# Most of the FFN's down projection by seven half-size products, its activation forms passed through DRAM

## The chip, the cores and the metric

The kernel runs on one core of a Trainium2 chip. The metric is the device time of one execution in microseconds; lower is better.

## The reference

One transformer layer over 512 tokens (T) of width 2048 (D) in float32, and a last RMSNorm. Only the second half matters here:

```python
x  = x + concat(oA, oB) @ W_out                  # two attention-like mixers, not changed
h  = RMSNorm(x)
a  = causal_conv3(h @ w_gate) + conv_b           # 2048 -> 5632
x  = x + (silu(a) * (h @ w_up)) @ w_down         # 5632 -> 2048
y  = RMSNorm(x)
```

## The kernel before

Everything is kept transposed, features on the 128 partitions and the 512 tokens along the free axis, so 2048 features are KT = 16 row blocks and 5632 are NF = 44. A float32 product is made of three matmuls on a split of each operand into a rounded part hi and a rest lo: hi·hi, hi·lo and lo·hi. The split of weights runs beside TensorE (PE): ScalarE (ACT) writes hi (`whi`, `fhi`), VectorE (DVE) subtracts it from the raw weights to get lo (`wlo`, `flo`).

The program is the mixers (to about 880 us of the span), the output projection, then three stages that the change touches.

**Gate and up.** For each of 44 row blocks f, gate and up together are a 2x2 product of half-size blocks, done with seven products in place of eight: sums of weight quarters (s1 to s4) meet seven forms of the activations (b11, n2, b21, t3, n1, n4, b22; `hforms`, held in SBUF). One product is 8 pairs of row blocks × 3 matmuls of 256 columns (L819 to L821), so a unit f has 168. Two of the weight sums are made by accumulating DMAs of POOL's queue (L765), two by DVE (L783), and `prepare` splits each of the seven weight tiles two products ahead. `glu(f)` runs the seven products, adds the partial results (L840 to L850), scales, convolves and gates (L851 to L858), splits the 128x512 activation (L860, L861) and stores both parts to DRAM (`actd`, L863, on the queue of SP).

**Down.** The activations come back from `actd` in four groups of GF = 11 row blocks (L886, POOL's queue). For each group and each of the 16 output blocks, `unit` runs 11 blocks × 3 matmuls of 512 columns (L201 to L203) into one PSUM tile, and DVE adds the tile to x1 in SBUF (L900). Weights `wdn` come on SP's queue (L142) and are split piece by piece (L149, L150).

**Late part and tail.** The last group of the last four output blocks is done with tokens on the partitions (L983 to L985), so that the final norm can start; what follows the last matmul is one norm step (L955 to L974) and the output stores.

Each engine executes its instructions in program order; a tile framework places the waits. An instruction on SP or POOL that issues a DMA waits there for what the DMA needs, and all later issues of the queue stand behind it. A stage's SBUF is handed on when its pools are closed, so the first tile of the next stage waits for the last reader of the old one.

Of the kernel before, what the change touches and what calls it, by code (L numbers as in the profile page):

```python
# [22 lines left out]
GF = 11  # L23
NG = NF // GF
# [12 lines left out]
NPIECE_D = NF * KT * P // PIECE  # L37
QH = T // 2
KP = KT // 2
FORM = KP * P  # L40
LEAD = 2
DMA_SUMS = True
# [11 lines left out]
def tile_hymba_block(ctx: ExitStack, tc: tile.TileContext, xT, wst, wgu, wdn, wfb, consts, out, out_t):  # L54
# [71 lines left out]
    class Stream:  # L126
# [7 lines left out]
        def make(self):  # L134
# [531 lines left out]
    x1d = dr.tile([KT, P, T], F32, name="x1d")  # L666
    actd = dr.tile([NF, 2, P, T], F32, name="actd")
# [18 lines left out]
    forms = {n: [] for n in NAMES}  # L686
    acc2 = tt.tile([P, T], F32, name="acc2")

    def form(name, j, src):
        pool = tt if j < KP - 1 else tl  # L690
        hi = pool.tile([P, QH], F32R, name=f"{name}h{j}")
        lo = pool.tile([P, QH], F32R, name=f"{name}l{j}")
        s.activation(hi, src, AF.Copy)
        v.tensor_tensor(lo, src, f32(hi), op=ALU.subtract)
        forms[name].append((hi, lo))

    def pair_forms(j, ha, hb):
        b11, b12, b21, b22 = ha[:, 0:QH], ha[:, QH:T], hb[:, 0:QH], hb[:, QH:T]
# [4 lines left out]
        form("b11", j, b11)  # L703
# [15 lines left out]
    def x1_out(d, ps):  # L719
# [3 lines left out]
        nc.sync.dma_start(out=x1d[d], in_=t)  # L723
# [10 lines left out]
    for d in range(WOPEN, KT):  # L734
        ps = MM()
        unit(ps, range(KT), os_)
        x1_out(d, ps)
    closed("wp", "wr", "pa")
    tl = opened("tl", 1)
    pair_forms(KP - 1, hg[-2], hg[-1])  # L740
    closed("xr")
    R2 = cp.tile([P, T], F32, name="R2", tag="R")
    nR2 = tl.tile([P, T], F32, name="nR2")

    def put2(u, r0, bc):
        s.activation(R2, bc, AF.Copy)
        s.activation(nR2, bc, AF.Copy, scale=-1.0)
# [3 lines left out]

    wf = opened("wf", 8)
    wh = opened("wh", LEAD + 2)
    gt = opened("gt", 1)
    ORDER = ("a11", "s2", "a12", "s3", "s1", "a22", "s4")
    raw = {}

    def W():
        return wf.tile([P, FORM], F32, name="wq", tag="wq")

    def load(f, name, q, q2=None):
        t = raw[f, name] = W()
        nc.sync.dma_start(out=t, in_=wgu[f, q])
        if q2 is not None:
            gp.dma_start(out=t, in_=wgu[f, q2], accum_op=ALU.add)  # L765

    def loads(f):

        if DMA_SUMS:
            load(f, "s1", 0, 1)  # L770
            load(f, "a11", 2)
            load(f, "s3", 0, 2)
            load(f, "a12", 3)
            load(f, "a22", 1)
        else:
            load(f, "a21", 0)
            load(f, "a22", 1)
            load(f, "a11", 2)
            load(f, "a12", 3)

    def add(f, name, x, y, into=None):
        t = raw[f, name] = W() if into is None else into
        v.tensor_tensor(t, raw[f, x], raw[f, y], op=ALU.add)  # L783

    def sums(f):
        if not DMA_SUMS:
            add(f, "s1", "a21", "a22")
            add(f, "s3", "a21", "a11", raw[f, "a21"])
        add(f, "s2", "s1", "a11")

    ready = {}
# [271 lines left out]
```

## Time and profile before

| | us |
|---|---|
| median of three runs | 2302.06 (2301.57 to 2303.62) |
| profiled execution, its own time | 2302.55 |
| span of the profiled execution | 2300.8 |
| gate and up, first to last matmul | about 905 to 1785 |
| down, from there to the last matmul | 1785 to 2290.8 |
| PE busy | 2273.4 (99%) |
| DVE, ACT, POOL busy | 1464.9, 939.2, 171.6 |

The profile is of one execution. Its span lies 1.75 us under that execution's own time, which holds what lies around the span; every "us from the start" is within the span. A busy PE is not PE at its peak: what a matmul costs is read from how many start in a stretch.

### The profile page before, as it was taken

The numbers are of one execution on the slowest core, as the hardware profiler recorded it, in microseconds if no ns is written. First come the engines' busy times: TensorE is split into PE (matmuls) and PEld (weight loads), VectorE is DVE, ScalarE is ACT, GpSimd is POOL, SyncE is SP. The second block draws the span as 40 slices with busy tenths as digits, with TensorE's granted clock in tenths as the row PEclk, the third lists the DMA queues.
The fourth block names the chain that finished last, engine by engine and source line by source line (L and its number), as shares of the span: only waits on it lengthen the run. The fifth ranks groups of instructions, "written<-read, shape, count | busy, mean of one in ns | idle before, by whom it ended". The sixth has DMA issues, their size and how long they took to land.

```text
span 2300.8 us, 34411 instructions
## 1 busy us (share of the span) xinstructions
PE 2273.4 (99%) x13662; PEld 2012.7 (87%) x13662; DVE 1464.9 (64%) x2194; ACT 939.2 (41%) x1484; POOL 171.6 (7%) x259
## 2 busy tenths in 40 slices
PE   8999999999999998999999999999999999999998
PEld 7888888788888887999999999999999788888886
DVE  6666467556457565888888888888887333333345
ACT  5333233334335454544444554454444222222234
POOL 4000000000000000000000000000000512000000
PEclk9999999999999999999999999999999999999999
DMA  5222322222222455877877887878784955223223
GB/s 177 83 83 83 100 74 96 74 83 80 86 83 74 142 163 177 226 212 207 216 215 214 212 212 209 216 200 222 208 217 136 375 198 196 92 97 99 85 100 110
DMA packets 112210, 352.67 MB, mean 153 GB/s; under 512 B 12816, under 2 KB 19088, under 8 KB 112048
## 3 DMA queue, kind: packets, MB, share of 16 engines
q1 hardware_dynamic: 89568, 272.67, 36.0%
q0 software_dynamic: 22336, 77.67, 15.4%
q8 instruction: 107, 1.75, 0.3%
q14 instruction: 55, 0.45, 0.1%
q10 hardware_dynamic: 144, 0.12, 0.0%
HBM read 318.96 MB, written 31.46 MB: 152 GB/s over the span
## 4 chain that ended last, share of the span: by engine, by line
PE 95%; DMA 2%; DVE 1%; issue 1%; ACT 0%; POOL 0%; DVEq 0%; ACTq 0%; POOLq 0%
PE pq L819 12%; PE pq L820 12%; PE pq L821 12%; PE mmt L201 9%; PE mmt L203 9%; PE mmt L202 9%; PE mxt L202 7%; PE mxt L201 7%; PE mxt L203 7%; PE mmt L286 2%; PE mmt L284 2%; PE mmt L285 2%; DMA ot<-actd 1%; DMA wq<-wgu 1%; DMA raw<-wdn 1%
## 5 line engine op out<-in xcount | busy, mean ns | idle before, releaser
L150 DVE TENSOR_TENSOR wlo<-raw,whi 128x512 fp32r<-128x512 f32 x453 | 316.3, 699 | 464.5 <-ACT whi L149 424.9
L149 ACT ACTIVATE whi<-raw 128x512 fp32r<-128x512 f32 x453 | 284.8, 630 | 686.3 <-PE mxt L202 322.2
L807 ACT ACTIVATE fhi<-wq 128x1024 fp32r<-128x1024 f32 x308 | 326.6, 1061 | 365.7 <-PE pq L820 323.0
L808 DVE TENSOR_TENSOR flo<-wq,fhi 128x1024 fp32r<-128x1024 f32 x308 | 376.3, 1222 | 58.2 <-ACT fhi L807 52.4
L201 PE MATMUL mmt<-at,whi 128*128 128x512 f32 x896 | 354.8, 396 | 0.0
L203 PE MATMUL mmt<-at,wlo 128*128 128x512 f32 x896 | 349.8, 390 | 0.0
L202 PE MATMUL mmt<-at,whi 128*128 128x512 f32 x896 | 349.3, 390 | 0.0
L201 PE MATMUL mxt<-ot,whi 128*128 128x512 f32 x660 | 262.2, 399 | 2.9 <-ACT whi L149 2.7
L202 PE MATMUL mxt<-ot,whi 128*128 128x512 f32 x660 | 261.8, 397 | 0.5 <-DMA ot<-actd 0.5
L203 PE MATMUL mxt<-ot,wlo 128*128 128x512 f32 x660 | 261.6, 397 | 0.5 <-DVE wlo L150 0.5
L203 PEld LDWEIGHTS mmt<-at,wlo 128*128 128x128 f32 x896 | 168.2, 188 | 35.9
L201 PEld LDWEIGHTS mmt<-at,whi 128*128 128x128 f32 x896 | 168.3, 188 | 34.9 <-issue 1.9
L202 PEld LDWEIGHTS mmt<-at,whi 128*128 128x128 f32 x896 | 168.4, 188 | 33.1
L201 PEld LDWEIGHTS mxt<-ot,whi 128*128 128x128 f32 x660 | 124.5, 189 | 34.8 <-ACT whi L149 2.9
L202 PEld LDWEIGHTS mxt<-ot,whi 128*128 128x128 f32 x660 | 124.6, 189 | 31.8 <-DMA ot<-actd 2.1
L203 PEld LDWEIGHTS mxt<-ot,wlo 128*128 128x128 f32 x660 | 124.7, 189 | 30.6 <-DVE wlo L150 1.0
L765 POOL DMA_DIRECT2D wq<-wgu x88 | 75.9, 862 | 782.1 <-DVE flo L808 388.1
L783 DVE TENSOR_TENSOR wq<-wq 128x1024 f32<-128x1024 f32 x88 | 107.5, 1222 | 3.5 <-DMA wq<-wgu 2.0
L286 PE MATMUL mmt<-wlo,at 128*128 128x512 f32 x256 | 100.6, 394 | 4.4 <-DVE wlo L150 4.4
L819 PE MATMUL pq<-b11h,fhi 128*128 128x256 f32 x352 | 100.2, 285 | 3.6 <-ACT fhi L807 3.6
L284 PE MATMUL mmt<-whi,at 128*128 128x512 f32 x256 | 101.7, 397 | 0.3 <-ACT whi L149 0.3
L821 PE MATMUL pq<-b11h,flo 128*128 128x256 f32 x352 | 99.9, 284 | 1.3 <-DVE flo L808 1.3
(303 smaller groups left out, 5067.7 us busy)
## 6 DMA issues: line engine op xcount, KB each, us to landing
wq<-wgu SPq DMA_DIRECT2D x220, 512.0 KB, 4.5
raw<-wst SPq DMA_DIRECT2D x143, 512.0 KB, 3.5
wq<-wgu POOLq DMA_DIRECT2D x88, 512.0 KB, 7.3
raw<-wdn SPq DMA_DIRECT2D x87, 512.0 KB, 3.5
ot<-actd POOLq DMA_DIRECT2D x88, 256.0 KB, 6.6
actd<-ah SPq DMA_DIRECT2D x44, 256.0 KB, 3.2
actd<-al SPq DMA_DIRECT2D x44, 256.0 KB, 3.0
xt<-xT SPq DMA_DIRECT2D x16, 256.0 KB, 5.3
```

Of the source, the lines that this page charges most:

```text
L149: s.activation(hi, src, AF.Copy)
L150: v.tensor_tensor(lo, src, f32(hi), op=ALU.subtract)
L201: pe.matmul(ps, lhsT=a, rhs=xh[:, ts], start=(first and i == 0), stop=False)
L202: pe.matmul(ps, lhsT=a, rhs=xl[:, ts], start=False, stop=False)
L203: pe.matmul(ps, lhsT=b, rhs=xh[:, ts], start=False, stop=(last and i == n - 1))
L284: pe.matmul(pss[i], lhsT=xh[:, ts], rhs=hi, start=(k == 0), stop=False)
L286: pe.matmul(pss[i], lhsT=xh[:, ts], rhs=lo, start=False, stop=(k == KT - 1))
L807: s.activation(hi, t, AF.Copy)
L808: v.tensor_tensor(lo, t, f32(hi), op=ALU.subtract)
L819: pe.matmul(ps, lhsT=a, rhs=th, start=(first and j == 0), stop=False, **kw)
L820: pe.matmul(ps, lhsT=a, rhs=tl, start=False, stop=False, **kw)
L821: pe.matmul(ps, lhsT=b, rhs=th, start=False, stop=(j == KP - 1), **kw)
```

## The change

Of the 44 row blocks that down contracts over, the first 36 (18 pairs) are now done by the same seven-product scheme; the last FL = 8 stay as they were, in one group.

- The 18 pairs are four chunks of 5, 5, 4 and 4 pairs (`CHUNKS`). For each chunk, eight units (pairs of output blocks, in the order `DORDER`) run seven products of n pairs × 3 matmuls of 256 columns. A unit's result goes to DRAM by an accumulating DMA of POOL (`yd`), 32 of 512 KB.
- The seven forms of the activations are made during gate and up, one pair for every two units (`forms_out`: four DVE operations, then splits into hi and lo), and stored to `formd` in DRAM instead of `actd` (1.8 MB a pair where two units stored 1.05 MB before). In down, a form of a chunk is loaded into one of ten slots (`df`, NDF = 10, 1.31 MB with n = 5) by two DMAs of SP's queue: seven for the chunk that runs, and three of the next one after its second unit's products; the other four are loaded during its last unit.
- The RMS factor R2 is no longer multiplied into the up half in `glu`. So yd holds down's sum without it, and its start value is x1/R2: eight times a load of 512 KB into one of two buffers `xi`, two DVE operations of 512 columns, a store of 512 KB, all in the first chunk and on POOL's queue.
- Down's weights come as four raw quarters a unit (wd7, SP's queue); all four sums are made by DVE (L796). Raw weights are loaded a unit ahead, in gate and up staggered over the unit's products.
- The order of the seven products is another one (`ORDER`, `NAMES`), with p5 as one more copy by ACT.
- The first unit of gate and up has DVE sums, and its loads and splits stand ahead of the last `x1_out` of the output projection.
- The last part has 8 blocks where it had 11: 96 late matmuls. `norm` waits 11 steps of the late loop (of 8 steps a row) before its ones-matmul, and multiplies out of place, three operations per row as before.

The core of the diff, with the functions that it adds:

```diff
-GF = 11
-NG = NF // GF
+FL = 8
+CHUNKS = (5, 5, 4, 4)
+NDF = 10
+DORDER = (6, 7, 0, 1, 2, 3, 4, 5)
...
-    ORDER = ("a11", "s2", "a12", "s3", "s1", "a22", "s4")
-    NAMES = ("b11", "n2", "b21", "t3", "n1", "n4", "b22")
+    ORDER = ("a11", "s2", "s1", "a12", "s3", "s4", "a22")
+    NAMES = ("b11", "n2", "n1", "b21", "t3", "b22", "n4")
...
+            elif self.units[u][2]:
+                when = {0: ("a11", "s1"), 2: ("a12",), 3: ("s3",), 4: ("a22",)}
+                self.loads(u + 1, *when.get(i, ()))
...
+    def forms_out(p, r):
+        c, j = next((c, p - at) for c, at in enumerate(STARTS) if p < at + CHUNKS[c])
+        v.tensor_tensor(r[:, 4], r[:, 0], r[:, 1], op=ALU.subtract)
+        v.tensor_tensor(r[:, 1], r[:, 3], r[:, 1], op=ALU.subtract)
+        yield KP // 2
+        v.scalar_tensor_tensor(r[:, 5], r[:, 4], -1.0, r[:, 3], op0=ALU.mult, op1=ALU.subtract)
+        v.tensor_tensor(r[:, 6], r[:, 5], r[:, 2], op=ALU.add)
+        for a, b in ((0, 4), (4, 7)):
+            parts_out(r[:, a:b], b - a, lambda i: formd[c][a:b, i, :, j].rearrange("s p t -> p s t"))
+            yield 6 * KP
...
-        v.tensor_tensor(uu, uu, nR2, op=ALU.mult)
         s.activation(t, t, AF.Silu)
         v.tensor_tensor(uu, uu, t, op=ALU.mult)
-        for i, part in enumerate((hi, lo)):
-            nc.sync.dma_start(out=actd[f, i], in_=f32(part))
+        if f >= 2 * NPAIR:
+            parts_out(r[:, b:b + 2], 2, lambda i: actd[f - 2 * NPAIR, i])
+        elif f % 2:
+            start(forms_out(f // 2, r))
...
+    with tc.high_priority():
+        sv.loads(first, "a11", "a21", "a22", "a12")
+        sv.prepare(7 * first)
+        sv.prepare(7 * first + 1)
+    for i in range(7):
+        chunk[0][NAMES[i]] = load_form(0, NAMES[i])
...
+    def down(c, k):
+        m = DORDER[k]
+        def after(i):
+            if c == 0 and i == 0:
+                if k + 1 < KP:
+                    load_x1(DORDER[k + 1])
+            if c == 0 and i == 2:
+                xi = x1s.pop(m)
+                v.scalar_tensor_tensor(xi[:, 0], xi[:, 0], -1.0, rms, op0=ALU.mult, op1=ALU.mult)
+                v.tensor_tensor(xi[:, 1], xi[:, 1], rms, op=ALU.mult)
+                gp.dma_start(out=yd[m], in_=xi)
+            if c + 1 < len(CHUNKS) and k == (1 if i < NDF - 7 else KP - 1):
+                chunk[c + 1][NAMES[i]] = load_form(c + 1, NAMES[i])
+        o = G("o", (P, 2, T), bufs=2)
+        seven(*(G(n, (P, QH)) for n in ("p1", "p5", "u2", "u3")),
+              o[:, 0, L], o[:, 0, H], o[:, 1, L], o[:, 1, H], chunk[c], after)
+        gp.dma_start(out=yd[m], in_=o, accum_op=ALU.add)
...
-    for g in range(NG - 1):
-        nxt = []
-        for d in range(KT):
-            ps = MX()
-            unit(ps, range(GF), acts)
-            v.tensor_tensor(x1[d], x1[d], ps, op=ALU.add)
-            if d < GF:
-                nxt.append(acts_of((g + 1) * GF + d))
-        acts = nxt
...
-        start(norm(i, ps, ys, 6 if i < 3 else 0))
+        start(norm(i, ps, FL + 3 if i < 3 else 0))
```

The change moves instructions on the queues. The first place is SP's queue at the end of gate and up, where down begins. `actd<-ah` and `actd<-al` are the stores of the last units' activations, `raw<-wdn` loads down's weights. Before:

```order
478 L863 DMA actd<-ah 128x512 [waits DMAHW2_49,Activation_49]
479 L863 DMA actd<-al 128x512 [waits DMAHW3_49,DVE_49]
480 L142 DMA raw<-wdn 128x512 [waits DMAHW4_49,PE_49]
481 L142 DMA raw<-wdn 128x512 [waits DMAHW5_49]
482 L142 DMA raw<-wdn 128x1024 [waits DMAHW6_49,PE_49]
483 L142 DMA raw<-wdn 128x1024 [waits DMAHW7_49]
484 L142 DMA raw<-wdn 128x1024 [waits DMAHW4_49,DMAHW5_49,DMAHW0_49,DVE_49]
485 L863 DMA actd<-ah 128x512 [waits DMAHW1_49,Activation_49]
486 L863 DMA actd<-al 128x512 [waits DMAHW2_49,DVE_49]
487 L142 DMA raw<-wdn 128x1024 [waits DMAHW6_49,DMAHW3_49,DVE_49]
```

The same place of the changed kernel; `wq<-wd` loads the raw quarters of down's second unit, `df<-formd` are halves of the forms of the first chunk, of which 14 stand here in all (rows 487 to 502 without the two stores):

```order
485 L786 DMA wq<-wd 128x640 [waits DMAHW1_49]
486 L786 DMA wq<-wd 128x640 [waits DMAHW2_49]
487 L969 DMA df<-formd_5879 128x1280 [waits DMAHW3_49,PE_49]
488 L969 DMA df<-formd_5879 128x1280 [waits DMAHW4_49]
489 L889 DMA actd<-oh 128x512 [waits DMAHW5_49,Activation_49]
490 L889 DMA actd<-ol 128x512 [waits DMAHW6_49,DVE_49]
491 L969 DMA df<-formd_5879 128x1280 [waits DMAHW7_49,PE_49,Pool_49]
492 L969 DMA df<-formd_5879 128x1280 [waits DMAHW0_49]
493 L969 DMA df<-formd_5879 128x1280 [waits DMAHW1_49]
494 L969 DMA df<-formd_5879 128x1280 [waits DMAHW2_49]
```

Two units' weights and the first form now stand ahead of the last stores, and the other six forms behind them; the wait for PE in row 491 is for the last product of gate and up. Behind row 502 follow the weights of the third unit (4 DMAs), three forms of the second chunk (6) and the weights of the fourth unit (4).

The second place is POOL's queue in the same stretch of the changed kernel, where `xi` are the two buffers of the start values:

```order
143 L788 DMA wq<-wgu 128x1024 [waits DMAHW5_49,DMASW2_49,DVE_49]
144 L992 DMA xi<-x1d_5868 128x1024 [waits DVE_49]
145 L992 DMA xi<-x1d_5869 128x1024 [waits PE_49]
146 L1005 DMA yd_5876<-xi 128x1024 [waits DMASW0_49,DVE_49]
147 L1005 DMA yd_5877<-xi 128x1024 [waits DMASW3_49,DMASW1_49,DVE_49]
148 L992 DMA xi<-x1d_5862 128x1024 [waits DMASW4_49,DMASW2_49]
149 L992 DMA xi<-x1d_5863 128x1024 [waits DMASW5_49,DMASW3_49]
150 L1005 DMA yd_5870<-xi 128x1024 [waits DMASW6_49,DMASW4_49,DVE_49]
```

Where the queue brought back activations before (11 pairs of `ot<-actd`, then 16 `ot<-x1d`), it now runs a chain: a load, two DVE operations, a store, and only then the next load into the same buffer.

The third place is DVE in down's first unit of the changed kernel. `flo` is the lo part of a product's weights, `wq<-wq` a sum of weights, `u` a partial result:

```order
1913 L825 TENSOR_TENSOR flo<-wq,fhi 128x640 [waits PE_49,Activation_49]
1914 L1003 SCALAR_TENSOR_TENSOR xi<-xi,rms 128x512 [waits DMASW0_49,DVE_49]
1915 L1004 TENSOR_TENSOR xi<-xi,rms 128x512
1916 L796 TENSOR_TENSOR wq<-wq 128x640 [waits DMAHW7_49]
1917 L912 TENSOR_TENSOR u_18276<-p_18274,pq 128x256 [waits DMAHW6_49,PE_49,Activation_49]
1918 L825 TENSOR_TENSOR flo<-wq,fhi 128x640 [waits Activation_49]
1919 L1003 SCALAR_TENSOR_TENSOR xi<-xi,rms 128x512 [waits DMASW1_49]
1920 L1004 TENSOR_TENSOR xi<-xi,rms 128x512
1921 L825 TENSOR_TENSOR flo<-wq,fhi 128x640 [waits PE_49,Activation_49]
1922 L1003 SCALAR_TENSOR_TENSOR xi<-xi,rms 128x512 [waits DMASW4_49,DMASW2_49,DVE_49]
1923 L825 TENSOR_TENSOR flo<-wq,fhi 128x640 [waits PE_49,Activation_49]
```

The operations on `xi` stand between the splits, and the third of them (row 1922) waits for a load that itself waits for the first store; the split in row 1923 stands behind it.

## Rows read from the trace of the kernel before

**Rows 1.** The page's head: span, and busy time of each engine.

```profile
span 2300.8 us, 34411 instructions
PE 2273.4 (99%) x13662; PEld 2012.7 (87%) x13662; DVE 1464.9 (64%) x2194; ACT 939.2 (41%) x1484; POOL 171.6 (7%) x259
```

**Rows 2.** The chain that ended last, by engine.

```profile
PE 95%; DMA 2%; DVE 1%; issue 1%; ACT 0%; POOL 0%; DVEq 0%; ACTq 0%; POOLq 0%
```

**Rows 3.** Four stretches: gate/up, transition, down's start, down.

```profile
core 0: us, PE busy (x) PEld busy (x) DVE busy (x) ACT busy (x) POOL busy (x), PEclk, DMA share, GB/s
1200.00:1400.00 200.00, 200.00 (x1692) 200.00 (x1692) 167.82 (x202) 100.57 (x121) 17.28 (x20) 1.00 0.80 213
1785.20:1815.00 29.80, 25.95 (x92) 18.21 (x92) 12.27 (x19) 8.58 (x14) 18.18 (x35) 0.89 1.00 368
1795.00:1845.00 50.00, 49.34 (x206) 37.91 (x205) 15.49 (x24) 11.38 (x18) 29.06 (x55) 1.00 1.03 395
2000.00:2100.00 100.00, 100.00 (x430) 80.48 (x429) 32.80 (x49) 22.75 (x36) 0.54 (x1) 1.00 0.29 96
```

**Rows 4.** Timeline of PE, last late matmuls: start, duration, instruction.

```profile
2287.81 0.39 PE L985 MATMUL mxt<-ot 128*128 128x512 f32 x1
...
2290.53 0.39 PE L985 MATMUL mxt<-ot 128*128 128x512 f32 x1
```

**Rows 5.** Timeline of PE around down's start; idle time in brackets.

```profile
1784.98 0.28 PE L821 MATMUL pq<-b22h,flo 128*128 128x256 f32 x1
1787.94 0.50 PE L201 MATMUL mxt<-ot,whi 128*128 128x512 f32 x1 [2.67 <-ACT whi L149]
...
1791.46 0.63 PE L203 MATMUL mxt<-ot,wlo 128*128 128x512 f32 x1
1791.89 0.63 PE L201 MATMUL mxt<-ot,whi 128*128 128x512 f32 x1
...
1795.29 0.39 PE L203 MATMUL mxt<-ot,wlo 128*128 128x512 f32 x1
```

**Rows 6.** SP's timeline there: issue, wait included, of DMAs.

```profile
1791.43 0.33 SPq L863 DMA_DIRECT2D actd<-ah  x1
1792.16 0.33 SPq L863 DMA_DIRECT2D actd<-al  x1
```

**Rows 7.** DVE by shape, 1200 to 1400: count, busy, mean ns.

```profile
L808 DVE TENSOR_TENSOR flo<-wq,fhi 128x1024 fp32r<-128x1024 f32 x71 | 86.8, 1222 | 12.9 <-ACT fhi L807 11.6
L855 DVE SCALAR_TENSOR_TENSOR t<-a,con,t 128x510 f32<-128x510 f32 x10 | 7.5, 750 | 0.4
L851 DVE TENSOR_TENSOR a<-a,R 128x512 f32<-128x512 f32 x10 | 6.9, 692 | 0.3
L840 DVE TENSOR_TENSOR u<-p,pq 128x256 f32<-128x256 f32 x10 | 4.2, 421 | 0.0
```

**Rows 8.** DVE's timeline at down's start, operations back to back.

```profile
1790.05 0.69 DVE L858 TENSOR_TENSOR uu<-uu,t 128x512 f32<-128x512 f32 x1
1790.66 0.69 DVE L150 TENSOR_TENSOR wlo<-raw,whi 128x512 fp32r<-128x512 f32 x1
```

**Rows 9.** DMA issues of the whole run: KB each, median us to landing.

```profile
wq<-wgu SPq DMA_DIRECT2D x220, 512.0 KB, 4.5
wq<-wgu POOLq DMA_DIRECT2D x88, 512.0 KB, 7.3
ot<-actd POOLq DMA_DIRECT2D x88, 256.0 KB, 6.6
ot<-x1d POOLq DMA_DIRECT2D x16, 256.0 KB, 6.9
```

**Rows 10.** PE's timeline between the output projection and gate/up.

```profile
897.48 0.39 PE L203 MATMUL mmt<-at,wlo 128*128 128x512 f32 x1
...
904.72 0.58 PE L819 MATMUL pq<-b11h,fhi 128*128 128x256 f32 x1 [3.63 <-ACT fhi L807]
```

**Rows 11.** DVE's timeline at the very end.

```profile
2290.95 0.69 DVE L955 TENSOR_TENSOR ot<-ot,mxt 128x512 f32<-128x512 f32 x1 [1.52 <-PE mxt L985]
2294.97 1.88 DVE L974 TENSOR_TENSOR ot<-ot,mxt 128x512 f32<-128x512 f32 x3
```

More of the change, by code (lines that the diff above doesn't have):

```diff
@@ L740, in tile_hymba_block @@
+    sv = Seven()
+    for f in range(NF):
+        sv.add([wgu[f, q] for q in range(4)], KP, f > 0)
+    sv.loads(0, "a11", "a21", "a22", "a12")
+    sv.prepare(0)
+    sv.prepare(1)
+    x1_out(KT - 1, ps)
     pair_forms(KP - 1, hg[-2], hg[-1])
@@ L758, in W @@
[L758 to L779, printed above, removed]
@@ L811, in product @@
-    def product(g, ps, first=True):
-        prepare(g + LEAD)
-        hi, lo = ready.pop(g)
-        rhs = forms[NAMES[g % 7]]
-        for j in range(KP):
-            a, b = hi[:, j * P:(j + 1) * P], lo[:, j * P:(j + 1) * P]
-            th, tl = rhs[j]
-            kw = {"skip_group_check": not first}
-            pe.matmul(ps, lhsT=a, rhs=th, start=(first and j == 0), stop=False, **kw)
-            pe.matmul(ps, lhsT=a, rhs=tl, start=False, stop=False, **kw)
-            pe.matmul(ps, lhsT=b, rhs=th, start=False, stop=(j == KP - 1), **kw)
-            step()
+    gt = opened("gt", 1, "right")
@@ L851, in glu @@
+        seven(*(G(n, (P, QH)) for n in ("p1", "p5", "u2", "u3")), a[:, L], a[:, H], uu[:, L], uu[:, H], hforms)
         v.tensor_tensor(a, a, R2, op=ALU.mult)
@@ new lines, in tile_hymba_block, with load_form @@
+    opened("wh", LEAD + 2)
+    wr = opened("wr", 2)
+    wp = opened("wp", 3)
+    dt = opened("dt", 1, "right")
+    gt = opened("gt", 1, "right")
+    def load_form(c, name):
+        n = CHUNKS[c]
+        t = dt.tile([P, 2, max(CHUNKS), QH], F32R, name="df", tag="df", bufs=NDF)
+        for i in range(2):
+            nc.sync.dma_start(out=f32(t[:, i, 0:n]), in_=formd[c][SLOTS.index(name), i])
+        return [(t[:, 0, j], t[:, 1, j]) for j in range(n)]
+    chunk = [{} for _ in CHUNKS]
+    first = len(sv.units)
@@ L878, in O @@
+    load_x1(DORDER[0])
+    for c in range(len(CHUNKS)):
+        for k in range(KP):
+            if c + 1 == len(CHUNKS) and k + 1 == KP:
+                while ws.made < 3:
+                    ws.make()
+            down(c, k)
+    closed("gt", "dt")
+    pq = opened("pq", 33, "right")
+    yp = opened("yp", 1, "right")
     def O(dt=F32, shape=(P, T)):
         return pq.tile(list(shape), dt, name="ot", tag="q")
-    A = X = O
-    def acts_of(f):
-        parts = (O(F32R), O(F32R))
-        for i, part in enumerate(parts):
-            gp.dma_start(out=f32(part), in_=actd[f, i])
-        return parts
@@ new lines, in tile_hymba_block @@
+    for f in range(FL):
+        acts.append((O(F32R), O(F32R)))
+        for i, part in enumerate(acts[-1]):
+            nc.sync.dma_start(out=f32(part), in_=actd[f, i])
+    ys = []
+    for d in (12, 0, 4, 8):
+        y4 = yp.tile([P, 4, T], F32, name=f"y{d}")
+        for b in range(2):
+            gp.dma_start(out=y4[:, 2 * b:2 * b + 2], in_=yd[d // 2 + b])
+        ys.append(y4)
+    y12, *ys = ys
+    ng3 = sm.tile([P, KT], F32, name="ng3")
+    v.tensor_scalar_mul(ng3, con[:, C_G3:C_G3 + KT], -1.0)
```

360 lines of the change are left out of this document (226 added, 134 removed).

## The prediction

> **What bounds the kernel now.** I read first the page's head: PE is busy for 2273.4 us of a span of 2300.8, the next engine, DVE, for 1464.9 [rows 1]. The chain that ended last is PE for 95% and DMA for 2% [rows 2]. So time is gained by fewer or shorter matmuls, and lost where PE waits; I cost the change stage by stage in matmuls and then look for new waits. The stretches give the price of a matmul: in gate/up 1692 of 256 columns start in 200.00 us, 0.1182 us each; in down 430 of 512 columns in 100.00 us, 0.2326 each [rows 3]; the late ones start 12 steps apart in 2290.53 − 2287.81 us, 0.2267 each [rows 4]. In both stages PE never idles; DVE has 16% to spare in gate/up and the DMA engines 20% (share 0.80) [rows 3].
>
> The one place where down waits today is its start. The last matmul of gate/up starts at 1784.98, the next at 1787.94 after 2.67 us of waiting, and then matmuls come 0.43 us apart, half clock (1.2 GHz), until about 1795.3 [rows 5]. Of the 29.80 us from 1785.2, the 92 matmuls need 92 × 0.2326 = 21.4, so this transition costs 8.4 us, with DMA engines full (share 1.00 at 368 GB/s; 395 GB/s right behind) [rows 3].
>
> **The matmuls.** Before, down has 4 × 16 × 11 × 3 = 2112, of which 132 are late: 1980 × 0.2326 + 132 × 0.2267 = 490.5 us. After: 4 chunks × 8 units × 7 products, together 8 × 7 × 18 × 3 = 3024 of 256 columns, 12 × 8 × 3 = 288 of 512, and 96 late: 357.4 + 67.0 + 21.8 = 446.2. **Saved: 44.3 us**, if the new stage runs as tightly as gate/up does.
>
> **Down's start.** Now count what must land there. T0 is the end of gate/up. Weights of two units and the first form wait for nothing late and are there. Six forms (6 × 1.31 = 7.9 MB) stand in SP's queue behind the stores of the last activations, which today are issued 6.5 to 7.2 us after the last matmul's start [rows 5, 6]; after the change the chain is shorter (no multiplication by nR2, DVE freer), say T0 + 3.5. At 0.38 MB/us, between the 368 and 395 GB/s of the full engines [rows 3], they need 21 us alone. POOL's chain shares the engines: eight loads and eight stores of 0.52 MB, two buffers. A 0.26 MB load of POOL took 6.6 to 6.9 us there [rows 9], so a buffer's turn (load, two DVE operations, store) takes about 15 us, and some 4 MB move in 30 us. The sixth form lands at about T0 + 3.5 + (7.9 + 4)/0.38 = T0 + 35. A unit's matmuls take 105 × 0.1182 = 12.4 us; the queue lets PE work on the second unit's first products meanwhile (36 of its 105 matmuls in program order), so at T0 + 35 some 15 to 17 us of work have been done: loss 18 to 20 us. Then SP brings the third unit's weights, three forms of the second chunk (3.9 MB), and the fourth unit's weights. All that must land before the fourth unit starts is 14.9 MB by SP, up to 8.4 MB of the chain and 1.5 to 2 MB of accumulation: 25 MB at 0.38 are 66 us, where PE alone would be there at T0 + 37: loss 29. With 6 MB of chain by then it is 22. I take **24 us** (nearer to the count of all bytes, since nothing in these rows moves more), bounds 12 (395 GB/s, the chain held back by its own waits) to 35 (368 GB/s and everything before the fourth unit). Today's 8.4 go: **+15.6**.
>
> The Trainium skill (DMA: Bandwidth & Descriptors, Where 436 GB/s comes from) says that transfers between HBM and SBUF are bound at about 358 GB/s per core. This trace disagrees, with 395 GB/s over 50 us. By the page the 25 MB would take 70 us and the loss would be some 4 us more.
>
> **Steady units of down.** DVE per unit with n = 5: seven splits and four sums of 640 columns, five combinations of 256. No row has 640; between 512 (0.692) and 1024 (1.222) the records give 0.825 and 0.421 for 256 [rows 7]: 11.2 us. Back to back they start closer, 0.61 apart for 512 [rows 8] (88% of the record), hence 9.9. PE needs 12.4. The first chunk adds two operations on `xi` (1.3). With n = 4: 11 × 0.692 + 5 × 0.421 = 9.7 by records, 8.6 by starts, against 84 × 0.1182 = 9.9. It fits by either, closely by records: **0**, bound +13 (0.4 us in each of 32 units, if the order makes splits late). DMA with n = 4 per unit: 1.05 MB of weights, 0.92 of the next chunk's forms (7.3 MB over eight units), 0.52 of accumulation, taken twice since it reads and writes: 3.0 MB, at 0.38 8 us of 9.9.
>
> **Between chunks** four forms (5.2 MB, with n = 4: 4.2) load during the last unit. With that unit's weights and accumulations about 8.8 MB have 21 us before the last form is used; at 0.38 it takes 23 for n = 5. Three boundaries: **+3**, bounds 0 and 8.
>
> **From down's seven to its rows.** The 16 loads of activations (4.2 MB) wait for SBUF that the last product frees, and beside them run 4.2 MB of y on POOL. That is the transition of today again, 8.4 us [rows 3], with as many bytes for the first rows but weights made ahead: **+9**, bounds 5 and 13.
>
> **Gate/up.** Per unit DVE loses two operations of 512 and gains half of four of 256, one of 1024 and one of 768: +0.5 us on 16.8 (167.82/200 of 19.9), still under PE. DMA gains 0.39 MB on 213 GB/s × 19.9 us = 4.2: share 0.80 becomes 0.87 [rows 3]. **0**, bound +8. At its start PE idles from 897.5 to 904.72 today with the split last [rows 10]; the first loads then come earlier but wait for SBUF of the last out-projection weights, and three sums are DVE's: **0**, ±2.
>
> **Tail.** After the last matmul today's chain runs 2290.95 to 2300.8; its three last multiplications take 1.88 [rows 11]. The 11-step gap exceeds the eight steps of a row, so the third row's multiplications stand in DVE's order behind the fourth's: **+2**, bounds 0 and 3.
>
> **Sum**, on the profiled execution's own time of 2302.55: −44.3 + 15.6 + 3 + 9 + 2 = −14.7, so 2287.8; it lies 0.5 over the median of 2302.06, so 2287.4 for that median.
>
> **Rivals.**
> (a) The start is covered better than I count: POOL's chain runs late, so that forms have the engines alone. For it speaks that DVE's split order holds the chain at each round (its own work is under 1.5 us a turn [rows 7], the rest is waiting); against it that stores and loads are queued whenever a buffer is free. Loss 12 in place of 24, and boundaries 0: 2272.
> (b) DVE decides in down's units: records of 9.7 against 9.9 leave 2%, and a split stuck behind an `xi` wait (the third place of the order) holds all behind it. +13: 2300. It decides when a unit's DVE work passes PE's 9.9.
> (c) The slow side: the new form stores write pieces of 1 KB per row and partition, where `actd` wrote 2 KB. No row of this kernel has such a store. If they cost double, the store's share (0.92 MB a unit, 2.4 us) becomes 4.8 us and the DMA share 0.80 − 0.07 + 0.24 = 0.97 [rows 3], and accumulated weights, which land in 7.3 us even at 0.80 [rows 9], come late by about 1 us in each of 36 units: 2323. It decides once the share reaches 1.0 over a unit. In a sentence apart: the Trainium skill (DMA: Bandwidth & Descriptors, Specifications) puts the least piece for full rate at 512 B, by which this rival does nothing; no row here shows it.
> (d) The clock stays at half during the start. Each product of a unit is 1.8 us of matmuls and a form arrives every 3.4 to 5, so PE works in bursts; today after 2.67 us of waiting it ran at half clock for 7 us [rows 5]. While PE waits for forms anyway, slow matmuls cost little; the price is the work after the last form, up to two units at half speed before the full clock is back: +12, 2299. The Trainium skill (TensorE: Matmul & The Clock Gate, HAM oscillation) describes just this, short bursts between DMA waits that all run at 1.2 GHz; the trace of before agrees once, at 0.89 granted over the transition.
>
> **How the numbers follow.** My sum's case 0.50 (2276 to 2298), (a) 0.18, (b) 0.09, (c) 0.13, (d) 0.10. Predicted 2287.5. The range of 8 in 10 reaches over (a), (b) and (d), and half-way to (c) because several bounds may add up: 2264 to 2312. A measurement here can tell 0.2%, 4.6 us, from no change. Faster than 2297.5: 0.47 + 0.18 and a third of (b) and (d), 0.71. Within: 0.12, from the rest of (b), (d) and my case. Slower: 0.17, (c) and sums of upper bounds.
>
> **What would show it.** Down's units at 12.4 and 9.9 us with PE without gaps confirm the matmul term. At gate/up's end, waits of PE for `df` over 20 to 35 us with a DMA share of 1.0, then again before the fourth unit. At the rows' start about 9 us with waits for `ot<-actd`. Gate/up units still at 19.9 us with a share near 0.87, else (c). Splits waited for in down's units mean (b); full DMA throughput with low granted clock after the sixth form, (d). The prediction is wrong if gate/up gets longer, or if the start loses under 12 or over 35 us.

## The result, and the profile after

The changed kernel takes 2391.47 us (2389.7 to 2394.68, four runs), the kernel before 2302.47: a ratio of 1.0388 (1.037 to 1.0406). It is 89 us slower, where 14.7 us less was forecast. One of all the runs below, of `bboth`, ran at a mean granted clock of 0.72 and took 2903.73 us; the ratios leave it out. The page's head and chain of the changed kernel:

```profile
span 2390.1 us, 37853 instructions
PE 2284.5 (96%) x14958; PEld 2083.1 (87%) x14958; DVE 1645.3 (69%) x2567; ACT 1028.4 (43%) x1671; POOL 155.0 (6%) x209
...
PE 70%; DMA 14%; DVE 10%; issue 3%; ACT 2%; SPq 1%; DVEq 0%; ACTq 0%; POOL 0%; POOLq 0%
```

PE is still nearly always busy, but the chain has changed: 14% and 10% of it are now DMA and DVE, which had 2% and 1% [rows 1, 2]. A chain through DVE and DMA in stages that the forecast had as pure matmul time is the first sign. The stretches show where; they are gate/up, the four chunks of down (each ends where the last combination of its eighth unit starts on DVE, L928), and the rows done as before:

```profile
core 0: us, PE busy (x) PEld busy (x) DVE busy (x) ACT busy (x) POOL busy (x), PEclk, DMA share, GB/s
903.20:1807.00 903.80, 891.99 (x7394) 887.06 (x7394) 732.19 (x924) 450.71 (x574) 74.22 (x86) 1.00 0.82 222
1807.00:1952.00 145.00, 115.80 (x848) 111.26 (x849) 100.75 (x158) 51.36 (x88) 14.61 (x23) 0.89 0.77 261
1952.00:2072.00 120.00, 109.90 (x873) 106.72 (x871) 81.73 (x130) 48.22 (x86) 6.78 (x8) 0.99 0.66 203
2072.00:2168.00 96.00, 84.46 (x640) 81.75 (x641) 68.07 (x127) 37.62 (x75) 6.84 (x8) 0.95 0.63 186
2168.00:2267.50 99.50, 88.21 (x669) 84.73 (x667) 65.61 (x122) 38.06 (x77) 7.36 (x9) 0.95 0.55 147
2267.50:2377.00 109.50, 100.38 (x413) 76.89 (x414) 47.13 (x89) 39.99 (x72) 4.58 (x8) 0.94 0.47 155
```

Gate/up lasts 903.8 us where it was 880.6. Each chunk should last as long as its matmuls, 8 × 105 × 0.1182 = 99.3 us with five pairs and 79.4 with four, and lasts 144.7, 120.0, 96.5 and 99.4. DVE's busy share in the last two is only 0.7, and the DMA engines' 0.6: nothing is full, so these look like waits in sequence, not a lack of any engine. The granted clock of 0.95 in these stretches comes from short spells at 1.2 GHz that follow waits of PE, such as the 2.8 us before 2115.7 and the 3.0 us before 2155.8.

What DVE does in the third unit of the last chunk of the changed kernel (start, duration, instruction, idle time before it):

```profile
2209.85 0.68 DVE L796 TENSOR_TENSOR wq<-wq 128x512 f32<-128x512 f32 x1
2210.45 0.41 DVE L928 TENSOR_TENSOR o<-u,pq 128x256 f32<-128x256 f32 x1
2210.79 1.29 DVE L825 TENSOR_TENSOR flo<-wq,fhi 128x512 fp32r<-128x512 f32 x2
2211.99 0.41 DVE L912 TENSOR_TENSOR u<-p,pq 128x256 f32<-128x256 f32 x1
2212.32 1.29 DVE L825 TENSOR_TENSOR flo<-wq,fhi 128x512 fp32r<-128x512 f32 x2
2218.32 1.42 DVE L796 TENSOR_TENSOR wq<-wq 128x512 f32<-128x512 f32 x2 [4.71 <-DMA wq<-wd]
2219.66 0.69 DVE L825 TENSOR_TENSOR flo<-wq,fhi 128x512 fp32r<-128x512 f32 x1
```

Two sums (L796) wait 4.71 us for raw weights, and the split that PE needs next (the last row) stands behind them. PE starts again right after that split:

```profile
2220.40 0.38 PE L847 MATMUL pq<-df,flo 128*128 128x256 f32 x1 [2.11 <-DVE flo L825]
```

The program's order, with the tiles' numbers, tells whose sums they are:

```
2258 L825 TENSOR_TENSOR flo_21493<-wq_21236,fhi_21492 128x512 [waits PE_49,Activation_49]
2259 L796 TENSOR_TENSOR wq_21653<-wq_21520,wq_21522 128x512 [waits DMAHW7_49,DMAHW6_49,DVE_49]
2260 L796 TENSOR_TENSOR wq_21520<-wq_21520,wq_21518 128x512 [waits DMAHW5_49,DVE_49]
2261 L825 TENSOR_TENSOR flo_21514<-wq_21375,fhi_21513 128x512 [waits PE_49,Activation_49]
```

The split in row 2261 opens the unit with raw weights 21375 and following; the sums before it belong to the unit after that one (21518 to 21522). In 18 of down's 32 units the first sum stands a whole unit early like this, seven splits ahead of the unit's own first one; in most others it stands three to six ahead. The loads were asked for only when DVE's earlier splits had freed the buffers. SP's queue issued them from 2209.96 to 2213.03, 5 to 8 us before the wait ended.

In gate/up of the changed kernel, DVE's timeline around a store of forms:

```profile
1040.21 1.22 DVE L888 TENSOR_TENSOR ol<-r,oh 128x1024 fp32r<-128x1024 f32 x1
1041.60 1.23 DVE L825 TENSOR_TENSOR flo<-wq,fhi 128x1024 fp32r<-128x1024 f32 x1 [0.17 <-ACT fhi L824]
1046.03 1.23 DVE L825 TENSOR_TENSOR flo<-wc,fhi 128x1024 fp32r<-128x1024 f32 x1 [3.20 <-ACT fhi L824]
1050.51 0.96 DVE L888 TENSOR_TENSOR ol<-r,oh 128x768 fp32r<-128x768 f32 x1 [3.25 <-DMA formd<-ol]
```

The second rest `ol` goes into the buffer whose first store has not landed. That store takes long, though the store of the hi parts, of the same size and in the same pieces, does not (DMA issues from 1000 to 1700: KB each, median us to landing):

```profile
formd<-ol SPq DMA_DIRECT2D x17, 512.0 KB, 8.0
formd<-oh SPq DMA_DIRECT2D x16, 512.0 KB, 4.4
```

And in down's first unit, an operation on `xi` stops DVE for 9.95 us, with the split of row 1923 of the front's third place behind it, for which PE then waits:

```profile
1825.00 0.83 DVE L825 TENSOR_TENSOR flo<-wq,fhi 128x640 fp32r<-128x640 f32 x1
1835.77 0.69 DVE L1003 SCALAR_TENSOR_TENSOR xi<-xi,rms 128x512 f32<-128x512 f32 x1 [9.95 <-DMA xi<-x1d]
1836.38 0.82 DVE L825 TENSOR_TENSOR flo<-wq,fhi 128x640 fp32r<-128x640 f32 x1
```

and of PE's timeline there, the same columns:

```profile
1837.26 0.58 PE L847 MATMUL pq<-df,flo 128*128 128x256 f32 x1 [7.26 <-DVE flo L825]
```

So my theory was: three waits in DVE's fixed order (the sums, the single store buffer, xi), not engines or transfers that are too slow. The rival was the transfers.

### The profile page after: what moved, and what is told of

The parts are those of the page before. It is cut to its first block, busy times and chain, and to the rows that moved or that the text cites. A ratio compares the mean times of both kernels' runs of the same rounds, so it can differ in the third digit from the quotient of the medians.

```text
span 2390.1 us, 37853 instructions
## 1 busy us (share of the span) xinstructions
PE 2284.5 (96%) x14958; PEld 2083.1 (87%) x14958; DVE 1645.3 (69%) x2567; ACT 1028.4 (43%) x1671; POOL 155.0 (6%) x209
## 4 chain that ended last, share of the span: by engine, by line
PE 70%; DMA 14%; DVE 10%; issue 3%; ACT 2%; SPq 1%; DVEq 0%; ACTq 0%; POOL 0%; POOLq 0%
PE pq L847 10%; PE pq L846 10%; PE pq L845 10%; PE mmt L204 9%; PE mmt L206 9%; PE mmt L205 9%; DMA wq<-wd 6%; DVE flo L825 3%; DMA df<-formd 3%; DMA formd<-ol 2%; PE mmt L289 2%; PE mmt L287 2%; PE mmt L288 2%; DVE wq L796 2%; ACT fhi L824 1%
## 5 line engine op out<-in xcount | busy, mean ns | idle before, releaser
L824 ACT ACTIVATE fhi<-wq 128x1024 fp32r<-128x1024 f32 (+2 forms) x400 | 331.4, 846 | 414.7 <-PE pq L846 246.0
L825 DVE TENSOR_TENSOR flo<-wq,fhi 128x1024 fp32r<-128x1024 f32 (+2 forms) x400 | 379.0, 959 | 37.3 <-ACT fhi L824 29.7
L847 PE MATMUL pq<-df,flo 128*128 128x256 f32 x1008 | 295.8, 294 | 37.6 <-DVE flo L825 37.4
L845 PE MATMUL pq<-df,fhi 128*128 128x256 f32 x1008 | 295.1, 293 | 13.8 <-DMA df<-formd 6.1
L846 PE MATMUL pq<-df,fhi 128*128 128x256 f32 x1008 | 292.6, 291 | 11.5 <-DMA df<-formd 11.5
L825 DVE TENSOR_TENSOR flo<-wc,fhi 128x1024 fp32r<-128x1024 f32 x132 | 161.5, 1224 | 122.4 <-ACT fhi L824 106.4
L847 PEld LDWEIGHTS pq<-df,flo 128*128 128x128 f32 x1008 | 198.3, 197 | 44.8 <-DVE flo L825 44.7
L824 ACT ACTIVATE fhi<-wc 128x1024 fp32r<-128x1024 f32 x132 | 139.7, 1058 | 212.7 <-DVE wc L796 146.6
L845 PEld LDWEIGHTS pq<-df,fhi 128*128 128x128 f32 x1008 | 198.3, 197 | 18.6 <-issue 7.0
L846 PEld LDWEIGHTS pq<-df,fhi 128*128 128x128 f32 x1008 | 198.7, 197 | 13.3 <-DMA df<-formd 13.3
L796 DVE TENSOR_TENSOR wq<-wq 128x640 f32<-128x640 f32 (+2 forms) x129 | 97.8, 758 | 86.5 <-DMA wq<-wd 85.3
L847 PE MATMUL pq<-n1h,flo 128*128 128x256 f32 x352 | 100.4, 285 | 7.9 <-DVE flo L825 7.9
```

Source lines behind the costliest of these rows:

```text
L796: v.tensor_tensor(t, x, y, op=ALU.add)
L824: s.activation(hi, t, AF.Copy)
L825: v.tensor_tensor(lo, t, f32(hi), op=ALU.subtract)
L845: pe.matmul(ps, lhsT=a, rhs=th, start=(first and j == 0), stop=False, **kw)
L846: pe.matmul(ps, lhsT=a, rhs=tl_, start=False, stop=False, **kw)
L847: pe.matmul(ps, lhsT=b, rhs=th, start=False, stop=(j == n - 1), **kw)
```

## The experiments

**Three waits, one at a time and together.** In `sums` the two sums may not be issued ahead of the last split of the unit before theirs. In `bufs` the forms are stored in four steps with two buffers. In `xi` the operations on xi stand behind a split two products ahead. `all3` has the three.

```diff
-                self.sum(u, "s1", "a21", "a22")                                          # sums
-                self.sum(u, "s3", "a21", "a11", into="a21")
+                with tc.issue_after(self.last) if u > NF else nullcontext():
+                    self.sum(u, "s1", "a21", "a22")
+                    self.sum(u, "s3", "a21", "a11", into="a21")
...
-            v.tensor_tensor(lo, t, f32(hi), op=ALU.subtract)
+            self.last = v.tensor_tensor(lo, t, f32(hi), op=ALU.subtract).ins             # sums, xi
...
-            t = G("oh" if i == 0 else "ol", (P, 4, QH), F32R)[:, 0:n]
+            t = G("oh" if i == 0 else "ol", (P, 2, QH), F32R, bufs=2)[:, 0:n]    # bufs
...
-        for a, b in ((0, 4), (4, 7)):
+        for a, b in ((0, 2), (2, 4), (4, 6), (6, 7)):
...
-            yield 6 * KP
+            yield 2 * KP
...
-                v.scalar_tensor_tensor(xi[:, 0], xi[:, 0], -1.0, rms, op0=ALU.mult, op1=ALU.mult)   # xi
-                v.tensor_tensor(xi[:, 1], xi[:, 1], rms, op=ALU.mult)
+                with tc.issue_after(sv.last):
+                    v.scalar_tensor_tensor(xi[:, 0], xi[:, 0], -1.0, rms, op0=ALU.mult, op1=ALU.mult)
+                    v.tensor_tensor(xi[:, 1], xi[:, 1], rms, op=ALU.mult)
```

> Only DVE's order is changed: in down the sums s1 and s3 of a unit stand behind the last split of the unit before it, where the changed kernel has them a whole unit earlier, ahead of that unit's first split, waiting for raw weights that SP has just asked for. Theory (DVE blocked by its own order): the 20 to 30 us per chunk that DVE idles for the raw weights go, the units of the last three chunks come to about 13, 10.5 and 10.5 us (now 15.0, 12.1 and 12.4), and the time falls by 40 to 55 us, to about 2340. Rival (the transfers themselves are too slow, DMA engines or landing times): the wait moves from the sums to the splits, units stay over 12 us, and the time falls by less than 10.

Measured: 2348.3, 43 us less. The last three chunks take 103.9, 85.8 and 86.1 us, 40 us less together, and steady units 12.6 and 10.1. The wait of the sums is gone: of DVE's waits in the last chunk, first the changed kernel's longest, then the two longest of `sums`:

```profile
DVE wq L796 <- DMA wq<-wd: 20.1, 6, 4.7
```

```profile
DVE flo L826 <- ACT fhi L825: 6.5, 10, 0.8
DVE o L926 <- PE pq L848: 5.8, 2, 5.3
```

DVE now waits for PE and ACT, which is what an engine off the path looks like. The theory holds for the sums.

> In gate/up the parts of the seven forms are written out in four steps of two forms with two buffers for hi and two for lo, in place of two steps of four and three with one buffer each; the bytes and the 1 KB pieces stay. Theory (one buffer: DVE's second rest waits until the first store has landed, with the splits queued behind it): pairs of units go from 41.2 us to about 39.9, gate/up from 903.8 to some 882, the time falls by about 20, to 2371. Rival (c of the prediction: the 1 KB pieces load the DMA engines, and the accumulated weights come late): gate/up stays over 898, the time falls by less than 6.

Measured: 2384.59, 7 us less; gate/up 893.1, that is 10.7 us less: half of what the theory said and twice what the rival allowed. The pairs of units with stores come to 40.3 us, but a pair without any takes 40.1, where it was 39.8 before the change. So the store wait was worth some 11 us, and something else slows every matmul a little. The 11 us are rough: gate/up without this edit took 900.0 us in `sums`, 903.8 in the changed kernel and 911.7 in `xi`, and with it 892.8 to 895.7 in `all3` and the four runs that follow it. And the edit makes the steps smaller as well as giving them a second buffer; no run has one without the other.

> Only DVE's order is changed: the two operations on xi of a unit stand behind the split that is two products ahead of it, so that the chain of loads and stores of the start values is spread over the first chunk's units. Theory (DVE's splits stand behind waits of up to 10 us for xi): the first unit of down falls from 51.5 us to about 42 and the chunk from 144.7 to about 134, the time by 8 to 12, to 2380. Rival (the forms' bytes alone set the start): below 3 us.

Measured: 2385.40, 6 us less; the first unit 34.9 in place of 51.5, the first chunk 127.4 in place of 144.7. Gate/up, which the edit does not touch, was 8 us longer in that execution (911.7), so the stage is the better measure: 17 us for xi, all of it in the first unit.

> The three edits together (sums in their own unit, two buffers for the stored forms, xi spread). If they are three separate waits of DVE, the gains add up to 70 to 85 us, and the time is 2306 to 2321, still not clearly below the kernel before. If they hide one another or the DMA engines take their place, it stays over 2335.

Measured: 2317.49 (ratio to the kernel before 1.0058, 1.0041 to 1.0075): 74 us less. The three gains by themselves come to 56 us of time, or 68 by stages, so the waits did not hide one another; the first chunk falls by 25 us here, where `xi` alone took 17. What is left over the forecast: gate/up 893.7 (880.6 before), the first chunk 119.5, the others 104.8, 85.8, 86.2, the rows 110.

**What is left, by stage.** Four runs on top of `all3`: `tiles` puts gate/up's forms into single tiles, `ends` asks for a chunk's last forms three products earlier and for y behind the activations on SP's queue, `pool` keeps each load of start values behind the accumulation of the unit two ahead, `best` has all.

```diff
+            hi, lo = (pool.tile([P, QH], F32R, name=f"{name}{x}{j}") for x in "hl")      # tiles
...
-            if c + 1 < len(CHUNKS) and k == (1 if i < NDF - 7 else KP - 1):
+            if c + 1 < len(CHUNKS) and k == 1 and i < NDF - 7:                            # ends, last forms
                 chunk[c + 1][NAMES[i]] = load_form(c + 1, NAMES[i])
+            if c + 1 < len(CHUNKS) and k == KP - 1 and i < 10 - NDF + 4:
+                chunk[c + 1][NAMES[i + NDF - 7]] = load_form(c + 1, NAMES[i + NDF - 7])
...
-            gp.dma_start(out=y4[:, 2 * b:2 * b + 2], in_=yd[d // 2 + b])
+            nc.sync.dma_start(out=y4[:, 2 * b:2 * b + 2], in_=yd[d // 2 + b])
...
+        load = gp.dma_start(out=x1s[m], in_=x1d[m])                                       # pool
+        if m != DORDER[0]:
+            tc.keep_in_program_order(load)
```

> On top of the three edits together, gate/up's activation forms lie in single tiles of 128x256, as before the change, in place of slices of tiles of seven. In the three edits together a matmul of gate/up starts every 119.45 ns, before the change every 118.3, and in down's forms, also slices of larger tiles, every 120.0. Theory (the layout of the moving operand costs it): gate/up returns to 118.3 ns, from 893.7 to about 885.5 us, the time by 8 to about 2309. Rival (the order of the seven products or the loads beside them): no change beyond 2 us.

> On top of the three edits together, the last four forms of the next chunk are asked for three products earlier, as soon as their slots come free, and the loads of y stand behind the activations on SP's queue in place of beside them on POOL's. Theory (what waits at the stage borders is the place of a load in its queue): the first two units of the last three chunks, now 30.0, 25.3 and 26.7 us where 25.2, 20.2 and 20.2 are steady, lose 2 to 4 us each, the stretch from the last unit to the last matmul falls from 110 to about 103, the time by 12 to about 2305. Rival (the bytes alone): below 3 us.

> On top of the three edits together, POOL asks for the start values of a unit only behind the accumulation of the unit two ahead of it, so that of the chain only two loads and stores fall into the time in which the six forms load. Theory (the chain's bytes compete with the forms): the first four units of down fall from 71.4 us to about 63, the time by 8, to about 2309. Rival (the forms' own 7.9 MB and their late start set it): below 3 us.

> All six edits together. If the three of this group act in different stages, their gains add up to 20 to 30 us on 2317, and the time is 2288 to 2298, for the first time below the kernel before (2303). If the layout does nothing it is about 2298 to 2302, not to be told from it.

Measured: 2318.68, 2320.24, 2317.99 and 2318.63 (best: ratio 1.007, 1.0056 to 1.0084). None does anything, as the rivals said: the first four units take 71.3 us in `all3` and in `pool`; in `ends` the first two units of the last three chunks take 32.3, 24.4 and 27.3 us (30.0, 25.3 and 26.7 in `all3`); a matmul of gate/up still takes 119.45 ns in `tiles`. But `pool` tests little. With the edit of `xi` in it, POOL asks in `all3` for only three loads and one store of start values during the first unit, and `pool` puts off one of these loads (from 1817.9 to 1832.8 us).

**The rate of a matmul.** One thing that still differed in every matmul was where its operands lie. In the built programs, the change's new tile rt2 of 16 bytes at the low end of SBUF had moved all split weights from 32 to 0 modulo 64 bytes, while the forms at the high end stayed at 32 (of gate/up's forms, one row block in eight lies at the low end and moved too). `left` and `right` are `all3` with a tile of 32 bytes (a pad) at the low or the high end; `bleft` and `bboth` are the kernel before with one at the low end and at both.

```diff
     con = cp.tile([P, N_C], F32, name="con")
+    pad = cp.tile([P, 8], F32, name="pad")
+    gp.memset(pad, 0.0)
```

> On top of the three edits together, a tile of 32 bytes per partition stands ahead of the others at the low end of SBUF. The change had put a tile of 16 bytes there (rt2), which moved the addresses of the split weights from 32 to 0 modulo 64, while the forms stayed at 32. Theory (the addresses of a matmul's operands set its rate): with both at 32 again, as before the change, a matmul of gate/up starts every 118.3 ns (now 119.45) and one of down's seven products too (now 120.0); gate/up falls by 8 us, down's units by 5, to about 2304. Rival (order of products, PSUM use): no change.

> On top of the three edits together, a tile of 32 bytes at the high end of SBUF puts the forms at 0 modulo 64, where the weights are already. Theory (addresses): the rate changes, to 118.3 ns or below if equal alignment is what counts, and possibly well below if 64 bytes are; the time is 2304 or less. Rival: no change from 2317.

> The kernel before, with a tile of 32 bytes ahead of the others at the low end of SBUF, and nothing else. Theory (addresses): weights at 0, forms at 32 as after the change, so its gate/up falls to 119.45 ns a matmul, 8 us longer, 2310. Rival: no change from 2302.

> The kernel before with such a tile at each end, so that weights and forms of gate/up both lie at 0 modulo 64. Theory (addresses): 118.3 ns or less, 2302 or less; if 64-byte alignment itself counts, all stages gain and it is clearly below 2302. Rival: no change.

Measured: `left` 2306.96 (1.0017, 1.0008 to 1.0027) and `right` 2306.46 (1.0015, 1.0005 to 1.0024), each 11 us less than `all3`; `bleft` 2311.65 (1.0038, 1.0023 to 1.0053), 9 us more than the kernel before, with nothing else changed; `bboth` 2297.56 (0.998, 0.9971 to 0.999), 5 us less than the kernel before. The stretches of [rows 3] again, first in `bleft`, then in `bboth`:

```profile
1200.00:1400.00 200.00, 200.00 (x1677) 200.00 (x1676) 166.25 (x200) 99.56 (x120) 17.26 (x20) 1.00 0.81 213
2000.00:2100.00 100.00, 100.00 (x430) 80.45 (x429) 33.34 (x49) 22.12 (x35) 0.54 (x1) 1.00 0.30 98
```

```profile
1200.00:1400.00 200.00, 200.00 (x1689) 200.00 (x1688) 167.58 (x203) 99.58 (x120) 17.27 (x20) 1.00 0.81 215
2000.00:2100.00 100.00, 100.00 (x439) 82.05 (x438) 33.24 (x49) 22.90 (x37) 0.54 (x1) 1.00 0.30 98
```

At the same clock, 1677 matmuls of gate/up start in `bleft` where 1692 did, and every steady unit takes 20.07 us for 19.88, which over 44 units makes 8 of the 9 us. Down has 430 in `bleft` as before, though its weights have moved, and 439 in `bboth`, where the activations have moved too. So the theory's rule, equal residues, fits the products of 256 columns and not those of 512. `bboth` is the one version with the whole result that beats both kernels.

**The bytes at the borders.** Two runs on top of `right`. In `half` the hi part of each form and last activation also stands in for lo, so half of these loads and bytes, and the rests' share of the result, are left out; `first4` has the chunks 4, 5, 5, 4.

```diff
-        for i in range(2):
-            nc.sync.dma_start(out=f32(t[:, i, 0:n]), in_=formd[c][SLOTS.index(name), i])
-        return [(t[:, 0, j], t[:, 1, j]) for j in range(n)]
+        nc.sync.dma_start(out=f32(t[:, 0, 0:n]), in_=formd[c][SLOTS.index(name), 0])
+        return [(t[:, 0, j], t[:, 0, j]) for j in range(n)]
...
-CHUNKS = (5, 5, 4, 4)
+CHUNKS = (4, 5, 5, 4)
```

> On top of right: only the hi part of each form and of each of the last activations is loaded in down, and it stands in for the rest lo too (so half of these bytes and loads are left out, and the rests' share of the result; the matmuls are the same in number and size). Theory (the bytes set the stage borders): the first chunk falls from 118.6 us to about 106, the three later ones from 103.5, 84.3 and 84.6 to about 100, 80 and 80, the last stretch from 109.4 to about 101; the time by some 30 us to about 2275. Rival (places in the queues, landing times, the late start): less than 10 us in all.

> On top of right: chunks of 4, 5, 5 and 4 pairs in place of 5, 5, 4, 4, all work as before. Theory (bytes): the first chunk has 20% less to load before it can run, its excess over its matmuls falls from 20 to about 15 us, the borders change by 2 at most: 2301 to 2303, equal to the kernel before. Rival: no change from 2306.

Measured: `half` 2279.01, 27 us less than `right`, nearly what the bytes said. The stretches of `right` (the first chunk in three parts, the three other chunks, the start and the rest of the rows), then those of `half` (four chunks, rows):

```profile
1790.20:1808.80 18.60, 9.44 (x46) 8.43 (x46) 12.56 (x17) 5.32 (x9) 1.63 (x3) 0.72 0.84 317
1808.80:1840.00 31.20, 28.05 (x229) 27.25 (x230) 23.91 (x37) 12.91 (x23) 3.20 (x6) 1.00 1.03 396
1840.00:1908.80 68.80, 68.30 (x577) 67.89 (x577) 64.14 (x104) 33.06 (x58) 10.04 (x16) 1.00 0.93 281
1908.80:2012.30 103.50, 100.11 (x834) 99.64 (x833) 82.12 (x129) 46.31 (x80) 6.83 (x8) 0.98 0.72 223
2012.30:2096.60 84.30, 82.10 (x683) 81.70 (x682) 70.35 (x129) 41.62 (x81) 6.84 (x8) 0.98 0.79 232
2096.60:2181.20 84.60, 80.70 (x663) 80.12 (x661) 66.05 (x122) 38.75 (x76) 7.36 (x9) 0.96 0.63 171
2181.20:2213.20 32.00, 23.06 (x66) 14.98 (x67) 4.73 (x8) 4.56 (x8) 4.57 (x8) 0.68 0.82 285
2213.20:2290.60 77.40, 77.40 (x350) 62.80 (x348) 42.48 (x82) 35.74 (x65) 0.00 (x0) 1.00 0.32 102
```

```profile
1792.00:1902.80 110.80, 104.29 (x851) 102.73 (x852) 100.82 (x158) 51.44 (x88) 14.89 (x23) 0.97 0.90 285
1902.80:2000.80 98.00, 98.00 (x835) 98.00 (x834) 82.14 (x130) 46.30 (x80) 6.84 (x8) 1.00 0.67 192
2000.80:2081.00 80.20, 80.20 (x684) 80.20 (x683) 70.01 (x130) 41.48 (x81) 6.85 (x8) 1.00 0.72 200
2081.00:2159.00 78.00, 78.00 (x663) 77.80 (x661) 65.83 (x122) 38.78 (x76) 7.38 (x9) 1.00 0.62 158
2159.00:2264.10 105.10, 99.53 (x415) 78.27 (x414) 47.30 (x89) 40.80 (x72) 4.57 (x8) 0.94 0.44 142
```

With half the loads and their bytes the three borders vanish: the later chunks take 98.0, 80.2 and 78.0 us, PE without idle time at full clock. The first chunk falls by 8 and the rows by 4, less than said. `first4` took 2308.34 (1.0025, 1.0015 to 1.0035), which its rival had: the first chunk is 100.0 for 79.4 of matmuls, an excess of 20 as before, and the second 106.7 for 99.3. A smaller first chunk has fewer bytes to wait for, but also less work to hide the next chunk's; my expectation had counted the first only. That this is why the excess stayed is an argument, not shown.

## Why the prediction was wrong

| term, us | forecast | measured |
|---|---|---|
| matmuls of down | −44.3 | −44.3, and +5 for their rate |
| down's start (first four units over their matmuls) | +24 | +38; +21 without the waits for xi |
| steady units of down | 0 | about +47; 40 of it went with `sums` |
| chunk borders | +3 | about +14 (in `right`) |
| start of the rows | +9 | about +14 |
| today's start of down | −8.4 | −8.4 |
| gate/up, and its start | 0 | +23.2 and −1.5 |
| tail | +2 | +2.8 |

The measured column adds up to about 90, of 89 measured.

**The step that failed** is the one on steady units: "It fits by either, closely by records: 0". It compared the busy time of DVE with PE's and so asked only whether the work fits. What decided was where DVE's fixed order put the sums: a unit early, behind loads asked for just before. It cost 40 us (`sums`). The order was at hand and showed it, in the numbers of the raw tiles. The bound that I gave (+13, "if the order makes splits late") named the mechanism but not its size: 0.4 us a unit, where DVE stood up to 4.7 us for one pair of sums. Rival (b) had the place right, DVE, and named the split behind a wait for `xi`; but it priced all of that at +13 with a chance of 0.09, and "it decides when a unit's DVE work passes PE's" is wrong: the busy shares of DVE stayed at 0.7.

**Gate/up** was costed at 0 for the same reason. The single buffer of `ol` was in the code. Its wait was worth about 11 us (`bufs`). Another 8 us came with the address of the weights, which nothing in the forecast covered (`bleft` repeats it in the old kernel). The other 4 us are a few long units that remain in `right`; their cause stays open. Rival (c) fell: `bufs` keeps the 1 KB pieces, and in `right` a pair of units with stores takes 40.1 us on average where one without takes 39.9; in the changed kernel the DMA share stayed at 0.82, and of two stores with the same size and pieces one landed after 8.0 us and the other after 4.4. The rule of the Trainium skill (DMA: Bandwidth & Descriptors, Specifications), that pieces of 512 B and more run at the full rate, is in accord with that, though no run here varied the piece alone.

**Down's start** came out near the forecast, in part by luck. The 24 us are 21 in `all3`, and `right` shows the DMA engines at a share of 1.03 and 396 GB/s for 31 us, so bytes were the right thing to count. The Trainium skill gives 358 GB/s as the bound there (DMA: Bandwidth & Descriptors, Where 436 GB/s comes from); the measurement is above it, and decides. But `half` takes only 10 us off the first four units (61.2 us for 71.2), and POOL's chain, which the sum took at 6 to 8.4 MB before the fourth unit, had moved or asked for 4.7 MB (five loads, four stores) when that unit ended in `all3`. Whether the chain competes for the engines, on which the choice between 12 and 35 hung, stays open, since `pool` put off a single load. What the sum left out were 17 us of DVE waiting for xi, which the third place of the order showed and only rival (b) named.

**Borders and rows** are the terms of bytes that I took too small: 14 and 14 for 3 and 9. `half` shows that the borders come from these loads, though not whether from their bytes or their number, which it halves together. The rows' start shrank by 4 us only with a quarter of its bytes away (half of 4.2 MB, the 4.2 MB of y stay), so what sets the rest of it stays open: y's loads, the slow clock (0.68 over its first 32 us), or the first landing.

**The tail and the matmul count** were right. Rival (a), 12 us at the start, did not come; (d) wanted a low clock after the sixth form; at the start of `right` it is low only in the first 19 us, where PE waits (0.72), and 1.00 from 1808.8 us on, before the first unit ends. In the changed kernel, with its longer waits, it is 0.89 over the first chunk and goes with them; what it cost by itself was not measured.

With these three waits gone and the addresses equal, the change is at 2306, within 0.2% of the kernel before. By the spans of `right` and the kernel before (2303.5 and 2300.8), the 44 us of matmuls and the 8.4 of the old start are used up by about 20 us at the first chunk, 14 at the borders, 14 at the rows, 5 in gate/up and 3 in the tail. `half` shows the loads of forms and last activations behind nearly all of the borders, but only 8 of the 20 and 4 of the 14 at the rows. Like has to be compared with like here: against `bboth`, whose operands lie as those of `right` do, the change is still 8.9 us slower (2306.46 and 2297.56).

## What to carry to other kernels

An engine that works in a fixed order is not off the path because its busy time fits: read, for each instruction of it that waits for a DMA, when that DMA was asked for and what stands behind the instruction; the tile numbers in the order tell when an operation belongs to a later round than its neighbours. A buffer that is written again by DVE after a store holds DVE for the landing time, so count stores among the waits too. And when a kernel gets slower all over by about a per cent, compare start-to-start times of the same instruction before looking for waits.

## What the runs showed of the hardware

- Where tiles start in SBUF changes how fast matmuls follow one another, by the operands' addresses modulo 64 bytes in the built programs. With weights at 0 and moving data at 32, a 128x256 matmul starts every 119.4 to 120.0 ns (`all3`, `bleft`); with both at 32 every 117.8 to 118.6 (`left`, the kernel before); with both at 0 the same (`right`, `bboth`). Every steady unit of gate/up takes 20.07 us in `bleft`, 19.93 in `bboth` and 19.88 without pads. A pad of 32 bytes at either end took 11 us off `all3`.
- The residues alone do not set it. In down of the kernel before, matmuls of 512 columns start 430 times in 100 us with both operands at 32 and with only the weights moved to 0 (`bleft`), and 439 times with both at 0 (`bboth`). Between 700 and 870 us, in the mixers, both operands lie at 32 in the kernel before and at 0 in `bleft` and `bboth`, and 768, 767 and 768 matmuls start. A pad moves every tile at its end of SBUF, those of DVE, ACT and the DMAs too, so that the matmul's own operands are the cause is not shown; and no run has weights at 32 and moving data at 0.
- In gate/up of the changed kernel a store of 512 KB in pieces of 1 KB landed after 8.0 us for `ol` and after 4.4 for `oh`; one of 256 KB in pieces of 2 KB had taken 3.0 to 3.3 before the change. So neither size nor pieces alone make the 8.0; what does was not separated.
- The DMA engines held 396 GB/s at a share of 1.03 for 31 us (`right`, from 1808.8 us).
